# Down projection of a hybrid decoder trunk: 8 of 22 k-pairs by seven block products instead of eight; masks and query slots in pages, x in DRAM during the FFN

## The chip, the cores and the metric

One Trainium2 chip, one core of it. The metric is the time of one execution in device microseconds, median of several runs. PE is TensorE, DVE is VectorE, ACT is ScalarE, POOL is GpSimd, SP is SyncE, which here only issues DMAs.

## The reference

Two layers on x (256 x 2048, f32): layer 0 has a dilated attention mixer, layer 1 a sparse attention mixer, and each ends with a SwiGLU feed-forward. D_FF is 5632. What the change touches most is the product with `w_down`:

```python
def swiglu(u, w_gu, w_down):
    gu = u @ w_gu
    return (jax.nn.silu(gu[..., :D_FF]) * gu[..., D_FF:]) @ w_down
# per layer: x = x + rmsnorm(mixer(rmsnorm(x, g[0])), g[1])
#            x = x + rmsnorm(swiglu(rmsnorm(x, g[2]), ffn_w_gu[l], ffn_w_down[l]), g[3])
```

## The kernel before

Every f32 product is done in three passes at PE's rounded f32 type: a number is split into `hi` (rounded) and `lo` (the rest), and hi·hi, lo·hi and hi·lo are summed in PSUM. The weights come in **units** of 128 x 1024 f32 (512 KB). A unit's way is the same everywhere: SP loads it (`dma_one`, L182), ACT writes hi (L193), DVE writes lo = raw - hi (L194), both in `split_one`, and PE reads hi and lo. `_unit_list` writes the order of all units down by hand. `take`, called by PE's loops for the next unit, keeps loads and splits ahead of PE in program order: up to `NRAW` loaded units that are not split yet, and splits up to `look` units ahead, if enough pages are free (`room`, `st["res"]`).

SBUF is handed out in **pages** of 4 KB per partition (`Pages`, `NPAGE` = 44), first in, first out: raw, hi, lo, the activations' hi/lo pairs (`XT`, one page for a k-pair, i.e. two k-tiles of 128), x (4 pages), the tail's products `og` (4) and gain rows `gb` (2). PSUM's 8 banks are handed out the same way.

Side work (attention heads, evacuations) is written as generators. `spawn` queues one, `tick` (one per product, two in `x_unit`) advances them, so their instructions fall between PE's products in program order.

In `ffn`, gate/up comes first: per f-pair two banks (token tile 0 and 1), 8 units each; `gu_evac` makes h = silu(g)·u, transposes it on PE (L808) and splits it into `hT` (L812, L813). The **down projection** then runs over 4 column chunks of 512. A chunk has 22 units, one k-pair each; `x_unit` does for each of 2 k-tiles and 2 token tiles three matmuls of 128x512 (L330 to L332), 12 for a unit, into two banks. `Tail.chunk` squares a chunk's result for the RMSNorm (L563) and multiplies it by the gain (L567). The last chunk holds back 4 units (`HOLD`), does them for token tile 0 and then for tile 1 (`Tail.last`), so that most of the end lies beside matmuls; then come the factor r_o (L358 on DVE, L359 on POOL) and the residual (L597). During chunk 3, `step_f` of layer 0 loads and splits the memory tokens for layer 1 (L383, L384). After layer 0's FFN `next_x` transposes the new x (L608) between the matmuls of `mem_k`.

The attention masks lie in a constant tile `cst` of 128 x 1848 f32, loaded once at the start; the query slots, `vc` and `pcT` are tiles of their own.

## Time and profile before

| | |
|---|---|
| median of 3 runs | 2556.78 us (2556.25 to 2558.38) |
| the profiled execution's own time | 2556.86 us |
| its span in the profile | 2555.1 us |
| PE, PEld, DVE, ACT, POOL busy | 2522.1, 2137.7, 1449.6, 1203.3, 58.5 us |
| DMA | 482.84 MB, 189 GB/s in the mean |

Busy time of PE counts each matmul from its issue to its last result, and these overlap (a 128x512 takes about 390 ns and the next starts 227 ns after it), so rates are read from starts, not from means. The chain of work that ended last lies to 93% on PE, 4% on DVE, 2% on ACT.

### The profile page before, as it was taken

The page shows a single profiled execution, that of the slowest core. Times are in us where ns is not written, and L with a number is a line of the kernel's source. Part 1 is how long each engine was busy: PE and PEld are TensorE (multiplying, and loading weights), DVE is VectorE, ACT ScalarE, POOL GpSimd, SP SyncE. Part 2 cuts the span into 40 slices and gives each one's busy share as a digit, 9 for nine tenths or more (in the row PEclk, how much of TensorE's full clock was granted, in tenths as well). Part 3 has the DMA queues.
Part 4 walks back from the last instruction along what each step waited for, and adds up shares of the span by engine and source line. Part 5 has one row for each costly group of instructions (what it writes and reads, how often), then busy time and mean ns, then how long its engine had stood idle before and what let it go on. Part 6 is the DMA issues. An engine that isn't in the chain of part 4 may idle for free.

```text
span 2555.1 us, 32090 instructions
## 1 busy us (share of the span) xinstructions
PE 2522.1 (99%) x12326; PEld 2137.7 (84%) x12326; DVE 1449.6 (57%) x1926; ACT 1203.3 (47%) x1704; POOL 58.5 (2%) x73
## 2 busy tenths in 40 slices
PE   8999999999999999999999999999899999999998
PEld 6899999988888888888888888888788888888887
DVE  8564655557445554444457866896544444444444
ACT  7444444456434444444445555565444444444442
POOL 5000000000000000000000000000000000000000
PEclk9999999999999999999999999999999999999999
DMA  8455555576555555566676675346455555556664
GB/s 305 148 181 173 166 166 173 172 246 223 177 183 181 185 187 170 173 209 192 194 233 216 220 245 193 116 142 235 158 175 181 181 174 173 181 173 219 193 190 156
DMA packets 136010, 482.84 MB, mean 189 GB/s; under 512 B 15408, under 2 KB 15408, under 8 KB 135856
## 3 DMA queue, kind: packets, MB, share of 16 engines
q1 hardware_dynamic: 131904, 468.67, 56.8%
q0 software_dynamic: 3232, 11.01, 1.3%
q8 instruction: 96, 1.57, 0.3%
q10 hardware_dynamic: 720, 1.11, 0.1%
q14 instruction: 58, 0.48, 0.1%
HBM read 478.63 MB, written 2.10 MB: 188 GB/s over the span
## 4 chain that ended last, share of the span: by engine, by line
PE 93%; DVE 4%; ACT 2%; issue 1%; DMA 0%; POOL 0%; SPq 0%; DVEq 0%; ACTq 0%; POOLq 0%
PE bk L331 23%; PE bk L332 23%; PE bk L330 23%; PE bk L295 12%; PE bk L297 6%; DVE lo L194 2%; ACT hi L193 1%; PE sk L808 1%; PE sk L500 1%; PE bk L939 1%; PE bk L938 1%; PE sk L540 0%; PE bk L294 0%; PE sk L1123 0%; DVE x L597 0%
## 5 line engine op out<-in xcount | busy, mean ns | idle before, releaser
L194 DVE TENSOR_TENSOR lo<-raw,hi 128x1024 fp32r<-128x1024 f32 (+2 forms) x899 | 1061.6, 1205 | 613.0 <-ACT hi L193 575.6
L193 ACT ACTIVATE hi<-raw 128x1024 fp32r<-128x1024 f32 (+2 forms) x899 | 906.9, 1039 | 499.5 <-PE bk L331 239.3
L330 PE MATMUL bk<-hi,xf 128*128 128x512 f32 x1408 | 554.0, 393 | 0.6 <-ACT xf L383 0.6
L332 PE MATMUL bk<-lo,xf 128*128 128x512 f32 x1408 | 549.3, 390 | 0.0
L331 PE MATMUL bk<-hi,xf 128*128 128x512 f32 x1408 | 548.9, 390 | 0.0
L295 PE MATMUL bk<-xT,hi 128*128 128x512 f32 x1104 | 398.7, 404 | 0.0
L332 PEld LDWEIGHTS bk<-lo,xf 128*128 128x128 f32 x1408 | 265.0, 188 | 55.7
L330 PEld LDWEIGHTS bk<-hi,xf 128*128 128x128 f32 x1408 | 265.1, 188 | 54.1 <-ACT xf L383 1.0
L331 PEld LDWEIGHTS bk<-hi,xf 128*128 128x128 f32 x1408 | 265.3, 188 | 53.5 <-DVE xf L384 0.2
L297 PE MATMUL bk<-xT,lo 128*128 128x256 f32 x1035 | 289.6, 280 | 0.0
L330 PE MATMUL bk<-hi,hT 128*128 128x512 f32 x704 | 274.1, 389 | 0.0
L332 PE MATMUL bk<-lo,hT 128*128 128x512 f32 x704 | 273.9, 389 | 0.0
L331 PE MATMUL bk<-hi,hT 128*128 128x512 f32 x704 | 273.9, 389 | 0.0
L295 PEld LDWEIGHTS bk<-xT,hi 128*128 128x128 f32 x1104 | 204.1, 188 | 39.8 <-issue 0.2
L297 PEld LDWEIGHTS bk<-xT,lo 128*128 128x128 f32 x1035 | 195.5, 189 | 3.1
L331 PEld LDWEIGHTS bk<-hi,hT 128*128 128x128 f32 x704 | 132.2, 188 | 27.6
L330 PEld LDWEIGHTS bk<-hi,hT 128*128 128x128 f32 x704 | 132.2, 188 | 27.3
L332 PEld LDWEIGHTS bk<-lo,hT 128*128 128x128 f32 x704 | 132.2, 188 | 27.3
L801 DVE SCALAR_TENSOR_TENSOR ev<-bk,r_f,ev 128x256 f32<-128x256 f32 x88 | 42.2, 483 | 136.7 <-ACT ev L799 127.8
L799 ACT ACTIVATE ev<-bk,r_f 128x256 f32<-128x256 f32 x88 | 41.5, 474 | 164.9 <-PE bk L332 163.8
L322 ACT ACTIVATE ev<-bk 128x256 f32<-128x256 f32 x93 | 35.5, 382 | 129.7 <-PE bk L295 129.6
L295 PE MATMUL bk<-kT,hi 128*128 128x512 f32 x256 | 91.6, 399 | 0.0
(210 smaller groups left out, 2486.6 us busy)
## 6 DMA issues: line engine op xcount, KB each, us to landing
...
```

The lines of the kernel that those rows point to most:

```text
L193: nc.scalar.activation(hi[1][:, s], r[:, s], AF.Copy)
L194: nc.vector.tensor_tensor(out=lo[1][:, s], in0=r[:, s], in1=hi[1][:, s].bitcast(F32), op=OP.subtract)
L295: mm(pt[:, :], lhsT=hi[:, ks], rhs=X.hl(kt), start=first, stop=last)
L297: mm(pt[:, S:], lhsT=lo[:, ks], rhs=X.part(kt, 0), start=False, stop=False)
L322: nc.scalar.activation(t1, pt[1][:, S:], AF.Copy)
L330: mm(p[:, :w], lhsT=xh, rhs=u[0][1][:, ws], start=f, stop=False)
L331: mm(p[:, :w], lhsT=xl, rhs=u[0][1][:, ws], start=False, stop=False)
L332: mm(p[:, :w], lhsT=xh, rhs=u[1][1][:, ws], start=False, stop=l)
L500: mm(s[:, o:o + n], lhsT=q[1][:, g, t * P:(t + 1) * P], rhs=k[1][:, g, :n], start=True, stop=True)
L799: nc.scalar.activation(g, pts[t][1][:, :S], AF.Silu, scale=r)
L801: nc.vector.scalar_tensor_tensor(h, pts[t][1][:, S:], r, g, op0=OP.mult, op1=OP.mult)
L808: nc.tensor.transpose(p[:, k * S + t * P:k * S + (t + 1) * P], hs[t][:, k * P:(k + 1) * P], ident)
```

## The change

**Seven products.** For the k-pairs 14 to 21 (`DN_S`) the 2 token tiles, 2 k-tiles and 2 column chunks of a pair of chunks (cp 0: chunks 0 and 1; cp 1: chunks 2 and 3) form a 2x2x2 block product, done in Winograd's form with 7 products of three matmuls instead of 8. The sums of activation blocks are made once per k-pair in `gu_evac` (`s_parts`), kept in `sp` pages and in the place of the block they replace. The sums of weight blocks are made by DVE at each use: of units a (chunk 2cp) and b (chunk 2cp+1), each with halves A and B (its two k-tiles), DVE forms b.A - a.A and b.B - b.A in a page `T13`, and from it a.A + b.B - b.A, and a.B less that, in a's own raw page, `T24`; both are split like units. Seven banks hold the products and an eighth (`Q`) the ordinary part of the block (chunk 1, tile 1). A k-pair of this kind is called a quad here: four `take`s (a, b, T13, T24), 21 matmuls. The other 14 k-pairs go as before (kinds a and b), woven between the quads; chunk pairs replace single chunks. `sums` and `block` put the products together on DVE (L1061 to L1067, L1074).

**Pages.** Masks, query slots, `vc` and `pcT` move into pages of the layer that needs them (`work_a`, `work_b`, `work_free`), loaded by POOL's queue; `cst` shrinks to 128 x 252. x is stored to DRAM after `next_x` of each FFN and loaded again in cp 1; `gb` takes one page at a time, `og` pages are taken when used; `NPAGE` is 48.

```diff
-NPAGE = 44
+NPAGE = 48
+DN_S = tuple(range(14, FT // 2))
+def _dn_steps(cp):
+    std = [u for u in range(FT // 2) if u not in DN_S]
+    a, b, q = [("a", u) for u in std], [("b", u) for u in std], [("S", u) for u in DN_S]
+    if cp == 0:
+        head, mix, tail = a[:4], [e for p in zip(a[4:], b) for e in p] + b[len(a) - 4:], []
+        tail, mix = mix[-4:], mix[:-4]
+    else:
+        head, mix, tail = a[:3], a[3:] + b[:6], b[6:]
+    return head + _weave(mix, q, 0) + tail
...
     def split_one():
...
+        if kd == "b":
+            ai, ra = kept["T24"]
+            hl = pages.get([P, UNIT], F32R, "hl", True)
+            split_ap(r[:, Bk], hl[1][:, A], hl[1][:, Bk])
+            ti, t = pages.get([P, UNIT], F32, "t13", True)
+            nc.vector.tensor_tensor(out=t[:, A], in0=r[:, A], in1=ra[:, A], op=OP.subtract)
+            nc.vector.tensor_tensor(out=t[:, Bk], in0=r[:, Bk], in1=r[:, A], op=OP.subtract)
...
+        if kd == "T13":
+            ai, ra = kept["T24"]
+            nc.vector.tensor_tensor(out=ra[:, A], in0=r[:, Bk], in1=ra[:, A], op=OP.add)
+            nc.vector.tensor_tensor(out=ra[:, Bk], in0=ra[:, Bk], in1=ra[:, A], op=OP.subtract)
         for s in halves(u, w):
+            split_ap(r[:, s], hi[1][:, s], lo[1][:, s])
...
     def next_x(tail, x, X, g, res, name, w=3):
...
+        if name == "f":
+            for i in range(4):
+                nc.sync.dma_start(out=x_out[i], in_=x[i][1])
+                pages.put(x[i][0])
...
+    def s_parts(p, H, u):
+        nc.scalar.activation(a21, A[:, 0, 1], AF.Copy)
+        tt(out=sv[:, 0], in0=A[:, 1, 1], in1=a21, op=OP.add)
...
+        for h, l, v in todo:
+            nc.scalar.activation(h, v, AF.Copy)
+            tt(out=l, in0=v, in1=h.bitcast(F32), op=OP.subtract)
...
+            def quad(u):
+                w = take(f"dn{l}")
+                prod("P1", act(2 * u, 0), w[0][1][:, A], w[1][1][:, A])
+                prod("P2", act(2 * u + 1, 0), w[0][1][:, Bk], w[1][1][:, Bk])
+                w = take(f"dn{l}")
+                prod("P3", sp[3], w[0][1][:, A], w[0][1][:, Bk])
+                w = take(f"dn{l}")
+                prod("P5", sp[0], w[0][1][:, A], w[1][1][:, A])
+                prod("P7", sp[2], w[0][1][:, Bk], w[1][1][:, Bk])
+                w = take(f"dn{l}")
+                prod("P6", sp[1], w[0][1][:, A], w[1][1][:, A])
+                prod("P4", act(2 * u + 1, 1), w[0][1][:, Bk], w[1][1][:, Bk])
...
+            def block(key, pre=None):
+                c, t, s_ = T["c"][key]
+                nc.vector.tensor_tensor(out=s_, in0=bk[key][1], in1=s_, op=OP.add)
+                free(key)
+                tail.rows(2 * cp + c, t, s_, pre)
...
+                    if 8 <= steps < 12:
+                        i = steps - 8
+                        x[i] = pages.get([P, 1024], F32, "x")
+                        nc.sync.dma_start(out=x[i][1], in_=x_out[i])
```

Three places where the order of instructions changes. PE in layer 0's down projection before, the first half of a unit (three matmuls per token tile; `bk` are the banks):

```order
L330 MATMUL bk_9302<-hi_9265,hT_6056 128x512
L331 MATMUL bk_9302<-hi_9265,hT_6056 128x512
L332 MATMUL bk_9302<-lo_9266,hT_6056 128x512
L330 MATMUL bk_9303<-hi_9265,hT_6056 128x512
L331 MATMUL bk_9303<-hi_9265,hT_6056 128x512
L332 MATMUL bk_9303<-lo_9266,hT_6056 128x512
```

PE in layer 0's down projection after, the third to sixth of the seven products of the first quad (`hl` holds hi and lo of half a unit, `sp` the sums of activations):

```order
L1019 MATMUL bk_9546<-hl_9469,sp_8232 128x512
L1020 MATMUL bk_9546<-hl_9469,sp_8232 128x512
L1021 MATMUL bk_9546<-hl_9469,sp_8232 128x512
L1019 MATMUL bk_9552<-hi_9489,hT_8188 128x512
L1020 MATMUL bk_9552<-hi_9489,hT_8188 128x512
L1021 MATMUL bk_9552<-lo_9490,hT_8188 128x512
L1019 MATMUL bk_9556<-hi_9489,sp_8232 128x512
L1020 MATMUL bk_9556<-hi_9489,sp_8232 128x512
L1021 MATMUL bk_9556<-lo_9490,sp_8232 128x512
L1019 MATMUL bk_9568<-hi_9507,sp_8232 128x512
L1020 MATMUL bk_9568<-hi_9507,sp_8232 128x512
L1021 MATMUL bk_9568<-lo_9508,sp_8232 128x512
```

Before, two banks take turns every three matmuls; now every product of a quad goes to a bank of its own, still three matmuls for each, and one product of the eight is gone.

DVE at the start of layer 0's down projection before: the last transposed k-pair and the splits of five units.

```order
L813 TENSOR_TENSOR hT_9283<-sk_9328,hT_9283 128x2x256
L194 TENSOR_TENSOR lo_9358<-raw_9312,hi_9357 128x1024
L194 TENSOR_TENSOR lo_9376<-raw_9314,hi_9375 128x1024
L194 TENSOR_TENSOR lo_9394<-raw_9341,hi_9393 128x1024
L194 TENSOR_TENSOR lo_9412<-raw_9361,hi_9411 128x1024
L194 TENSOR_TENSOR lo_9430<-raw_9379,hi_9429 128x1024
```

DVE there after: the first quad from its unit b on, and the next two units (`t` is the page T13, and `raw` on the left the page that becomes T24).

```order
L233 TENSOR_TENSOR hl_9469<-raw_9370,hl_9469 128x512
L248 TENSOR_TENSOR t_1371_9472<-raw_9370,raw_9368 128x512
L249 TENSOR_TENSOR t_1371_9472<-raw_9370 128x512
L258 TENSOR_TENSOR raw_9368<-t_1371_9472,raw_9368 128x512
L259 TENSOR_TENSOR raw_9368<-raw_9368 128x512
L233 TENSOR_TENSOR lo_9490<-t_1371_9472,hi_9489 128x1024
L233 TENSOR_TENSOR lo_9508<-raw_9368,hi_9507 128x1024
L233 TENSOR_TENSOR lo_9524<-raw_9388,hi_9523 128x1024
L233 TENSOR_TENSOR lo_9530<-raw_9442,hi_9529 128x1024
```

Before, a unit is one instruction of DVE; a quad, two units, is eight: a split of a (ahead of the piece), half a split of b, four block sums and two splits of the sums.

DVE at the end of the run before (layer 1's down projection), from the factor of token tile 0 to the last residual:

```order
L358 TENSOR_SCALAR s_20500<-ssq,s_20472 128x1
L567 TENSOR_TENSOR og_18922<-bk_20148,gb_18918 128x512
L597 SCALAR_TENSOR_TENSOR x_4896<-og_18921,r_o,x_4896 128x512 x2
L597 SCALAR_TENSOR_TENSOR x_4898<-og_18922,r_o,x_4898 128x512 x2
L358 TENSOR_SCALAR s_20537<-ssq,s_20472 128x1
L567 TENSOR_TENSOR og_18924<-bk_20149,gb_18918 128x512
L597 SCALAR_TENSOR_TENSOR x_4900<-og_18923,r_o,x_4900 128x512 x2
L597 SCALAR_TENSOR_TENSOR x_4902<-og_18924,r_o,x_4902 128x512
```

The same place on DVE after:

```order
L1074 TENSOR_TENSOR og_20949<-bk_20303,og_20949 128x512
L427 TENSOR_SCALAR s_21054<-ssq,s_21025 128x1
L671 TENSOR_TENSOR og_20949<-og_20949,gb_20234 128x512
L710 SCALAR_TENSOR_TENSOR x_20831<-og_20120,r_o,x_20831 128x512 x2
L710 SCALAR_TENSOR_TENSOR x_20849<-og_20949,r_o,x_20849 128x512 x2
L1074 TENSOR_TENSOR og_20950<-bk_20756,og_20950 128x512
L427 TENSOR_SCALAR s_21092<-ssq,s_21025 128x1
L671 TENSOR_TENSOR og_20950<-og_20950,gb_20234 128x512
L710 SCALAR_TENSOR_TENSOR x_20869<-og_20121,r_o,x_20869 128x512 x2
L710 SCALAR_TENSOR_TENSOR x_20916<-og_20950,r_o,x_20916 128x512
```

A sum of 128x512 (L1074) now stands ahead of each of the two factors, and it is what the squares on ACT wait for.

## Rows read from the trace of the kernel before

**Rows 1.** The page of the profile: the engines' busy times, and the granted TensorE clock in 40 slices (9 is 90% or more).

```profile
PE 2522.1 (99%) x12326; PEld 2137.7 (84%) x12326; DVE 1449.6 (57%) x1926; ACT 1203.3 (47%) x1704; POOL 58.5 (2%) x73
...
PEclk9999999999999999999999999999999999999999
```

**Rows 2.** Busy time of each engine by stretch (us from the span's start: its length; PE, PEld, DVE, ACT, POOL busy with counts of instructions; granted clock; DMA share; GB/s). Gate/up of layer 0; down projection of layer 0; what follows it; the output projection's end in layer 1; down projection of layer 1; the end.

```profile
626.00:1117.00 491.00, 489.93 (x2201) 405.26 (x2201) 243.03 (x242) 213.45 (x251) 1.66 (x3) 1.00 0.58 185
1117.00:1356.50 239.50, 239.50 (x1061) 198.38 (x1060) 124.16 (x121) 104.75 (x121) 5.40 (x10) 1.00 0.65 205
1356.50:1440.00 83.50, 80.82 (x459) 69.48 (x458) 65.73 (x96) 49.17 (x77) 4.04 (x9) 1.00 0.63 216
...
1800.00:1830.00 30.00, 22.35 (x98) 17.24 (x97) 17.33 (x36) 17.21 (x32) 1.62 (x3) 0.83 0.39 132
...
2306.00:2546.00 240.00, 240.00 (x1063) 198.76 (x1062) 114.71 (x103) 96.83 (x103) 1.09 (x2) 1.00 0.60 190
2546.00:2555.10 9.10, 0.54 (x3) 0.11 (x1) 3.89 (x5) 1.41 (x3) 2.24 (x2) 0.77 0.43 165
```

**Rows 3.** The waits of PE on other engines in the whole run (in total, times, the longest): the first, the second and the last of eleven.

```profile
PE sk L608 <- DVE x L597: 8.7, 5, 4.5
PE bk L330 <- ACT hi L193: 6.0, 1, 6.0
...
PE sk L1121 <- ACT pcT L1104: 0.3, 1, 0.3
```

**Rows 4.** PE's timeline in layer 0's down projection (start, length): the first and the last row of a run of 31 matmuls.

```profile
1344.01 0.39 PE L330 MATMUL bk<-hi,hT 128*128 128x512 f32 x1
...
1350.81 0.39 PE L330 MATMUL bk<-hi,hT 128*128 128x512 f32 x1
```

**Rows 5.** Instructions of layer 0's down projection by line (1117 to 1356 us: count, busy us, mean ns; idle time before them and what ended it).

```profile
L194 DVE TENSOR_TENSOR lo<-raw,hi 128x1024 fp32r<-128x1024 f32 x88 | 107.7, 1225 | 104.1 <-ACT hi L193 103.7
L193 ACT ACTIVATE hi<-raw 128x1024 fp32r<-128x1024 f32 x88 | 92.6, 1058 | 111.6 <-PE bk L331 97.9 <-PE bk L332 9.2 <-DMA raw<-in_dn 3.0
...
L384 DVE SCALAR_TENSOR_TENSOR mT<-xraw,gains,mT 128x256 fp32r<-128x256 f32 x16 | 7.1, 483 | 5.7 <-ACT mT L383 5.7
L567 DVE TENSOR_TENSOR og<-bk,gb 128x512 f32<-128x512 f32 x7 | 4.8, 690 | 2.1 <-ACT junk L563 2.0
```

**Rows 6.** DVE's instructions of the whole run by line and shape (count, busy us, mean ns, idle before).

```profile
L194 DVE TENSOR_TENSOR lo<-raw,hi 128x1024 fp32r<-128x1024 f32 x833 | 1003.4, 1226 | 613.0 <-ACT hi L193 575.6 <-PE bk L331 28.4 <-issue 1.4
...
L1057 DVE SCALAR_TENSOR_TENSOR bp<-cst,sk 128x128 f32<-128x128 f32 x24 | 5.7, 278 | 0.0
...
L194 DVE TENSOR_TENSOR lo<-raw,hi 128x512 fp32r<-128x512 f32 x2 | 1.3, 692 | 0.0
```

**Rows 7.** ACT's, in the same form.

```profile
L193 ACT ACTIVATE hi<-raw 128x1024 fp32r<-128x1024 f32 x833 | 857.0, 1055 | 499.5 <-PE bk L331 239.3 <-PE bk L332 213.3 <-DVE lo L194 17.0
...
L193 ACT ACTIVATE hi<-raw 128x512 fp32r<-128x512 f32 x2 | 1.2, 624 | 0.0
```

**Rows 8.** DVE's timeline in the B mixer: two splits of 128x1024 back to back (start, length of both).

```profile
1599.13 2.36 DVE L194 TENSOR_TENSOR lo<-raw,hi 128x1024 fp32r<-128x1024 f32 x2 [5.47 <-ACT hi L193]
```

**Rows 9.** DVE in the first 40 us by line, where POOL adds squares at the same time.

```profile
L384 DVE SCALAR_TENSOR_TENSOR mT<-xraw,gains,mT 128x256 fp32r<-128x256 f32 x16 | 13.2, 866 | 4.2 <-ACT mT L383 4.2
```

**Rows 10.** The busiest stretch for DMA, near the start, and one shortly after it (columns as in Rows 2).

```profile
16.00:24.00 8.00, 8.00 (x35) 6.04 (x34) 8.00 (x8) 6.36 (x11) 7.17 (x4) 1.00 1.03 410
...
80.00:100.00 20.00, 20.00 (x114) 17.61 (x113) 12.67 (x27) 10.86 (x25) 0.00 (x0) 1.00 0.40 125
```

**Rows 11.** The end of the run on PE, ACT, DVE and POOL, in that order (start, length, [idle before <- releaser]).

```profile
2546.15 0.39 PE L332 MATMUL bk<-lo,hT 128*128 128x512 f32 x1
...
2546.64 0.60 ACT L563 ACTIVATE junk<-bk 128x512 bf16<-128x512 f32 x1 [4.81 <-PE bk L332]
2547.13 0.19 ACT L563 ACTIVATION_READ_ACCUMULATOR junk<-bk 128x1 f32 x1
...
2542.81 2.74 DVE L597 SCALAR_TENSOR_TENSOR x<-og,r_o,x 128x512 f32<-128x512 f32 x4
2547.36 0.21 DVE L358 TENSOR_SCALAR s<-ssq,s 128x1 f32<-128x1 f32 x1 [1.80 <-ACT junk L563]
2547.49 0.68 DVE L567 TENSOR_TENSOR og<-bk,gb 128x512 f32<-128x512 f32 x1
2548.22 3.08 DVE L597 SCALAR_TENSOR_TENSOR x<-og,r_o,x 128x512 f32<-128x512 f32 x3
...
2547.65 0.54 POOL L359 TENSOR_TENSOR r_o<-s,mhalf 128x1 f32<-128x1 f32 x1 [4.87 <-DVE s L358]
```

**Rows 12.** PE's timeline behind layer 0's down projection.

```profile
1360.72 0.27 PE L608 MATMUL sk<-cst,x 128*128 128x128 f32 x1
1361.67 0.55 PE L608 MATMUL sk<-cst,x 128*128 128x128 f32 x3 [0.68 <-DVE x L597]
```

**Rows 13.** PE's timeline where it waits for the new x in layer 1: the wait, and the matmuls behind it.

```profile
1819.50 0.55 PE L608 MATMUL sk<-cst,x 128*128 128x128 f32 x3 [2.15 <-DVE x L597]
...
1820.60 0.63 PE L330 MATMUL bk<-hi,xf 128*128 128x512 f32 x1
1821.03 0.63 PE L331 MATMUL bk<-hi,xf 128*128 128x512 f32 x1
...
1824.00 0.40 PE L332 MATMUL bk<-lo,xf 128*128 128x512 f32 x1
```

More of the change, by code (lines that the diff above doesn't have):

```diff
@@ L92, in _gu_order, with _dn_order @@
     return [(f"gu{l}", c * n + u) for u in range(n) for c in range(2)] + [(f"gu{l}", i) for i in range(2 * n, FT * 4)]
+DN_S = tuple(range(14, FT // 2))
[8 more added lines that the diff above has]
+    return head + _weave(mix, q, 0) + tail
+def _dn_order(l):
+    n, o = FT // 2, []
+    for cp in range(2):
+        for kind, u in _dn_steps(cp):
+            ia, ib = 2 * cp * n + u, (2 * cp + 1) * n + u
+            if kind == "S":
+                o += [(f"dn{l}", ia, "a"), (f"dn{l}", ib, "b"), (f"dn{l}", ia, "T13"), (f"dn{l}", ia, "T24")]
+            else:
+                o.append((f"dn{l}", ia if kind == "a" else ib))
+    return o
 def _unit_list():
@@ L151, in drop, with drop_one @@
         self.gone += 1
+    def drop_one(self, k2):
+        self.pages.put(self.t[k2][0])
+        self.out.add(k2)
     def release(self):
-        while self.gone < len(self.t):
-            self.drop()
+        for k2 in range(self.gone, len(self.t)):
+            if k2 not in self.out:
+                self.pages.put(self.t[k2][0])
+        self.gone = len(self.t)
 @with_exitstack
@@ L211, in take @@
         for _ in range(0 if st["quiet"] else 2):
-            while st["dma"] < min(st["split"] + NRAW, n) and room(1):
+            while st["dma"] < n and len(raws) < NRAW and room(1):
                 dma_one()
@@ L215, in take @@
                 split_one()
-        while not st["quiet"] and st["dma"] < min(st["split"] + 4, n) and room(1):
+        while not st["quiet"] and st["dma"] < n and len(raws) < 4 and room(3):
             dma_one()
@@ L221, in give @@
     def give(u):
-        pages.put(u[0][0], True)
-        pages.put(u[1][0], True)
+        for e in u:
+            pages.put(e[0], True)
     side = []
@@ L253, in until @@
             n += 1
-            assert n < 1000
+            assert n < 1000, (sorted(banks.live.values()), len(pages.free) + len(pages.own), [e[0].__name__ for e in side], [e[0].gi_frame.f_lineno for e in side])
     def drain():
@@ L480, in mem_head, with work_page, work_a, work_b @@
         pages.put(ti)
+    work, mask, qs = [], {}, {"n": 0, "s": []}
+    def work_page(name):
+        work.append(pages.get([P, 1024], F32, name))
+        return work[-1][1]
+    def work_a():
+        m0, m1 = work_page("mask"), work_page("mask")
+        nc.gpsimd.dma_start(out=m0[:, :768], in_=a["mask_a"][:, :768])
+        nc.gpsimd.dma_start(out=m1[:, :384], in_=a["mask_a"][:, 768:])
+        mask.update({0: m0[:, :384], 1: m0[:, 384:768], 2: m1[:, :384]})
+        qs["s"] = [m0[:, 768:], m1[:, 384:640], m1[:, 640:896]]
+    def work_b():
+        m, q, r = work_page("mask"), work_page("q"), work_page("pcT")
+        nc.gpsimd.dma_start(out=m[:, :NMASK_B], in_=a["mask_b"])
+        mask["b"], mask["vc"] = m, m[:, 512:]
+        nc.gpsimd.memset(m[:, 512:], 0.0)
+        nc.gpsimd.memset(r[:, :768], 0.0)
+        mask["pcT"] = [r[:, i * S:(i + 1) * S] for i in range(3)]
+        qs["s"] = [q[:, i * S:(i + 1) * S] for i in range(4)] + [r[:, 768:]]
+    def work_free():
+        while work:
+            pages.put(work.pop()[0])
+    def q_slot():
+        qs["n"] += 1
+        return qs["s"][qs["n"] % len(qs["s"])]
     sl_a = slopes(len(GROUPS) * AH)
@@ L599, in release @@
         def release(self):
-            for i, _ in self.og:
+            for i, _ in self.og.values():
                 pages.put(i)
@@ L608, in transposed @@
                 nc.tensor.transpose(p[:, k * S + t * P:k * S + (t + 1) * P], x[2 * t + kt // 8][1][:, hs], ident)
+    x_out = [dram.tile([P, 1024], F32, tag=f"x{i}", name=f"x{i}") for i in range(4)]
     def next_x(tail, x, X, g, res, name, w=3):
@@ L813, in gu_evac @@
         nc.vector.tensor_tensor(out=hp[:, :, 1, :], in0=pv, in1=hp[:, :, 0, :].bitcast(F32), op=OP.subtract)
+        if f2 in DN_S:
+            Sp[f2] = yield from s_parts(p, H, f2)
         banks.put(b)
@@ L841, in ffn @@
+        pair(0)
+        pair(1)
+        tail.finish()
         H.release()
+        st["look"] = 4
         return tail
@@ L919, in k_win @@
         return k_page(1)[:, 272 + g * S:272 + (g + 1) * S] if g < 2 else k_page(2)[:, g - 2, :]
[L922 to L926 removed]
+    work_b()
+    vc = mask["vc"].rearrange("p (g d) -> p g d", g=BG)
     def cmp_unit(i, u):
```

296 lines of the change are left out of this document (230 added, 66 removed).

## The prediction, made before the change was run

> **What bounds the kernel now.** I read the page first: PE is busy for 99% of the span at the full granted clock, DVE for 57% and ACT for 47% [rows 1]. The table by stretch says the same where the change lies: in both down projections PE is busy for the whole stretch, 239.50 of 239.50 us and 240.00 of 240.00, at clock 1.00, while DVE has 124.16 and 114.71 us of work, ACT 104.75 and 96.83, and DMA is 65% and 60% busy [rows 2]. The list of waits agrees: PE waits for others some 24 us in the run, 8.7 of them at the residual x between stages and 6.0 at the very start; none of the eleven kinds of wait is for a split of a down projection unit [rows 3]. The splits of those 88 units follow their producers at leisure: DVE idles 104 us before them for ACT's hi, and ACT 98 us before hi for PE, which has yet to free a page [rows 5]. So the down projection lasts as long as its matmuls need to issue, and a matmul taken away there is time taken away, provided that DVE and ACT still deliver.
>
> **What a matmul is worth.** Its row says 389 ns, but that is a latency. From 1344.01 to 1350.81 us there are 30 starts, so one costs 6.80 / 30 = 0.2267 us [rows 4]. I take this.
>
> **Step 1, the removed products.** 2 layers x 2 chunk pairs x 8 quads, one product of three matmuls less in each: 96 matmuls, 96 x 0.2267 = **-21.8 us**, all of it on PE's path. The other products keep their shape (128x128 weights, 512 columns) and their three matmuls for one bank, as before. The Trainium skill, page "TensorE: Matmul & The Clock Gate", section "Back-to-back issue gap", gives another price: 2.5 ns plus columns over 2.4 GHz, 215.8 ns, for a lone matmul and some 131 ns sustained, by which the 96 would be worth 20.7 or 12.6 us and the time would be 2537.6 or 2545.7 us. The measured distance in this very stage is above both, and decides.
>
> **Step 2, what DVE has to do for a quad.** Splits of 1024 columns at 1.226 us and of 512 at 0.692 us [rows 6]; the four block sums have the nearest row in that 512-wide split, too (f32, two operands in SBUF). A quad: 3 x 1.226 + 0.692 + 4 x 0.692 = 7.14 us, against 2.45 us for its two units before. These durations overlap in a queue: two 1024-wide splits take 2.36 us together, the second 1.14 us behind the first [rows 8]; by the same 0.09 us a 512-wide one is about 0.60, and the quad 6.42 us. PE needs 21 x 0.2267 = 4.76 us for the quad, so DVE falls behind by 1.7 to 2.4 us in it, and must make that up in the ordinary units woven between, where PE needs 12 x 0.2267 = 2.72 us and DVE 1.14 to 1.23.
> In cp 0 there are 20 units to 8 quads, 2.5 for one: PE 11.56 us, DVE 9.3 to 10.2 (80 to 88%). In cp 1 there are two: PE 10.20, DVE 8.7 to 9.6 (85 to 94%). ACT stays low: 5 x 1.055 + 0.624 = 5.9 us of 10.20 [rows 7]. Splits stand three to five units ahead of PE in program order; a part that is split five ahead may begin when PE begins the fifth before it. With two units, a, b, T13, T24 begun by PE at 0, 2.72, 5.44, 6.80, 7.48, 8.84 us and so on from 10.20, DVE may begin the next b at 7.48, has it (1.80 us) at 9.3 and T13 (2.34) at 11.6, and PE wants them at 17.0 and 17.7: some 6 us to spare. So I cost this at nothing. Its cover is the two ordinary units between quads.
> Tightest are two places. At the start of cp 1 the four blocks of cp 0 come first, each a sum and a product with the gain at 0.690 us [rows 5], 5.5 us; then DVE needs 1.23 + 2.07 + 2.61 us to have T13 ready, 11.4 us in all at full durations, and PE wants it after four units, P1, P2 and P3, 10.88 + 2.04 = 12.9 us: 1.5 us to spare. In layer 0's cp 1 the memory tokens add 2 x 0.483 us [rows 5] at every second step; in the worst period, around the last quad, two such steps make 9.6 + 1.9 = 11.5 us against 10.20, which the lead of about 6 us pays.
>
> **Step 3, the sums of activations.** `s_parts` adds per k-pair four 128-wide DVE operations on PSUM (0.278 us each by the nearest row [rows 6]) and splits of 128 and 384 columns, at most 0.3 and 0.7: some 2.1 us, in a stretch of gate/up in which DVE works 243 of 491 us [rows 2]. Hidden; if not, the first quad waits, since the last k-pair's sums are needed only at the eighth.
>
> **Step 4, the ends.** The last product is now followed by a sum of 128x512 on DVE before ACT can square: 0.690 us [rows 5] plus one hand-over of 0.04 (ACT's accumulator row ends at 2547.32, DVE's next begins at 2547.36 [rows 11]). In layer 1 this lies on the path: **+0.7 us**. Token tile 0 gets the same, but its residuals end at 2545.55 now and would at 2546.3, before the last matmul's end at 2546.54 [rows 11]. In layer 0 PE already waits 0.68 us for the residual [rows 12], so the same sum adds **+0.7 us** there.
>
> **Step 5, DMA and pages.** Weight traffic is the same. x goes out and back in each layer: 4 x 2.1 MB. The worst stretch is the one of cp 1 in which x comes back: two quads and two units, 15.0 us, with six unit loads and four of x of 0.52 MB and two of memory tokens of 0.26, 5.8 MB or 385 GB/s. The queues have moved 410 [rows 10], and three or four raw units lie ready in front of it. Nothing. SP waits for x to be final before it stores it and for a freed page before it loads it, with raw loads queued behind; but at both places the loads for the next eight or so units have been issued. Nothing. `cst` is 0.82 MB smaller at the start: at 410 GB/s the loads behind it come 2.0 us sooner, but DVE works 8.00 of 8.00 us there [rows 10] and is what PE waits for. Between 0 and -2.0 us I take 0. The masks come later, when DMA is 40% busy [rows 10]. The 48 pages less 2 or 3 for masks leave every other stage at least as many as it had.
>
> **The sum.** -21.8 + 0.7 + 0.7 = -20.3 us. The profiled execution took 2556.86 us, its span 2555.1 and 1.8 around it, and 2556.86 - 20.3 = 2536.6; it lies 0.08 above the median, so **2536.5 us**. Faster or slower by 0.2%, 5.1 us, is what a measurement of this kernel can tell from no change.
>
> **Rivals.**
> *Part of it comes back as waits in the quads* (10%). For it: the starts of cp 1 with 1.5 us to spare, DVE at 94% behind them. Against it: the lead elsewhere. A wait costs more than itself: behind an idle 2.15 us at 1819.50, eight matmuls from 1820.60 to 1824.00 were 0.43 us apart instead of 0.23 [rows 13], the lower clock, 1.6 us. Waits of 1 to 2 us with that, at two to four places: 2541 to 2549 us.
> *The distance between matmuls grows in the products* (5%, about no change). If a product of its own bank, weights and moving tile costs more than the alternation of two banks now, the 32 x 21 = 672 matmuls need 0.259 us instead of 0.227 to eat the 21.8 us: 2552 to 2562. Against it: two banks already change every three matmuls at 0.2267.
> *DVE becomes the bound, slower* (5%). Two SBUF operands are what the block sums read; an operation of that engine with f32 operands in SBUF took 0.866 us in the first 40 us, where POOL computes beside it, against 0.483 later [rows 5, 9]. In the down projection POOL works 5.4 of 239.5 us [rows 2], so there is no such neighbour. It would decide from where a quad costs DVE more than 10.20 - 2 x 1.14 = 7.9 us, 0.9 for each 512-wide operation. At 1.14, as for twice the width, a quad is 9.1 us, and a period 11.4 in cp 1 and 12.0 in cp 0: 16 x 1.2 + 16 x 0.4 = 26 us lost, 2563 us, and up to 50 more if PE drops to the lower clock at every quad.
> *The clock falls in the quads, slower* (2%). At the lower spacing of 0.427 us [rows 13] the 672 matmuls would take 134 us more, 2671. The whole run holds 1.00 wherever PE is fed, and drops only behind waits [rows 1, 2]. The same page of the Trainium skill, section "A second HAM failure mode: psum-queue depth-cycling", reports a kernel that cycled through PSUM banks and lost its clock between groups of matmuls, which is what seven banks in turn look like; this trace has no such case.
>
> **How the numbers follow.** The forecast has 78%, and alone spans 2534.5 (the start gains its 2.0 us) to 2541. The range 2534 to 2549 takes in the first rival; 12% lie above. Faster: 78 + 10 = 88%; within 0.2%: 5%; slower: 5 + 2 = 7%.
>
> **What would show it.** PE has 12,326 - 96 = 12,230 matmuls, still 0.227 us apart in the quads; each down projection lasts about 11 us less (228.6 us) with PE idle under 1 us and clock 1.00. DVE's busy time grows by 32 x 4.7 for quads, some 22 for sums and blocks and 34 for `s_parts`, to about 1660 us, ACT's by less than 100. The first wait behind the last matmul is 0.7 us longer. Waits of PE for lo (the split) or for a block sum's T13 or T24 in the down projections, or clocks under 1.00 there, would prove a rival right. If the down projections shrink by 22 us and the time does not, another stage has paid.

## The result, and the profile after

The changed kernel takes **2532.91 us** (median of four runs, 2531.84 to 2533.12) against 2557.5 for the kernel before (four runs, 2556.25 to 2558.38): ratio 0.9903, 95% interval 0.9886 to 0.9921. Its profiled execution took 2532.82 us with a span of 2531.0. The forecast was 2536.5, the range 2534 to 2549: faster as forecast, but by 24.0 us between the two profiled executions instead of 20.3, and 1.1 us below the range.

The page of the changed kernel, which answers to [rows 1]: 96 matmuls fewer, DVE 170 us busier, ACT 51, and the clock as before.

```profile
PE 2498.8 (99%) x12230; PEld 2119.4 (84%) x12230; DVE 1619.9 (64%) x2254; ACT 1254.8 (50%) x1828; POOL 59.2 (2%) x74
...
PEclk9999999999999999999999999999999999999999
```

Its busy times by stretch, with the columns of [rows 2]: gate/up of layer 0, the two halves (cp 0, cp 1) of the down projection of layer 0, those of layer 1, the end.

```profile
625.20:1115.70 490.50, 489.43 (x2199) 404.81 (x2198) 254.69 (x291) 218.81 (x278) 1.67 (x3) 1.00 0.56 189
1115.70:1222.00 106.30, 106.30 (x472) 88.03 (x471) 91.15 (x103) 59.06 (x65) 0.00 (x0) 1.00 0.63 200
1222.00:1344.60 122.60, 122.60 (x542) 101.51 (x542) 108.04 (x134) 69.52 (x92) 5.71 (x10) 1.00 0.69 240
2291.60:2398.00 106.40, 106.40 (x473) 88.08 (x472) 87.92 (x101) 58.57 (x65) 0.00 (x0) 1.00 0.62 203
2398.00:2520.70 122.70, 122.70 (x542) 101.31 (x540) 98.43 (x115) 57.80 (x72) 1.40 (x2) 1.00 0.55 192
2520.70:2531.00 10.30, 0.04 (x1) 0.00 (x0) 4.69 (x7) 1.44 (x3) 2.66 (x2) 0.68 0.50 170
```

Both down projections are 229 us long, PE never idles in them, the clock stays at 1.00, and DVE is 80 to 88% busy. PE's waits in the whole run (as [rows 3]; first, second, last) hold nothing of the down projections, as before:

```profile
PE sk L721 <- DVE x L710: 7.0, 3, 3.3
PE bk L399 <- ACT hi L232: 6.3, 1, 6.3
...
PE sk L1421 <- DVE bp L1367: 0.3, 1, 0.3
```

PE's timeline in a quad of layer 1 (as [rows 4]; start, length): from the third product of a quad to the second product of the unit behind it eighteen matmuls start in 4.08 us, 0.2267 apart; each product of the quad goes to a bank of its own. The first of them, one in the middle, and the one behind them:

```profile
2330.18 0.39 PE L1019 MATMUL bk<-hl,sp 128*128 128x512 f32 x1
...
2332.22 0.39 PE L1019 MATMUL bk<-hi,sp 128*128 128x512 f32 x1
...
2334.26 0.39 PE L1019 MATMUL bk<-hi,hT 128*128 128x512 f32 x1
```

The quads did what was forecast; the rest came from stages that the quads don't touch. The stages in us, each from its first matmul's start in PE's timeline to the next one's, the first from the span's start, the last from the last matmul's start to the span's end (e1 to e12 are the experiments below, 44p and so on their numbers of pages; A mixer is the attention mixer of layer 0, kv and b_q the two parts of layer 1's):

```
stage                before   e12   after    e1   e2(44p) e5(46p) e9(47p)  e10     e7
start                 59.29  58.80  58.43  58.88   58.22   58.57   58.51  58.25  58.19
A mixer              470.09 470.20 470.54 470.61  470.54  470.54  470.73 470.56 470.73
a_out, memory values  97.11  97.11  96.24  96.23   96.24   96.23   96.23  97.20  96.22
gate/up 0            490.62 490.62 490.51 490.59  491.06  490.57  490.56 490.58 490.58
down 0               239.82 239.83 228.95 239.82  231.10  230.00  229.95 228.94 229.44
its end, mem. keys 1  27.42  27.40  27.84  27.07   28.19   28.19   27.84  27.85  27.09
kv                   165.65 165.68 164.77 164.79  167.07  165.48  164.77 164.76 164.86
b_q (mixer 1)        152.46 152.48 151.21 151.21  195.18  151.20  153.59 151.21 151.20
b_out and its end    104.82 104.81 103.77 103.40  104.32  104.90  103.45 103.76 103.77
gate/up 1            499.27 499.06 499.38 499.05  499.40  499.38  499.29 499.40 499.25
down 1 to last matm. 239.60 239.60 228.72 239.60  232.82  229.73  228.72 228.72 229.22
end                    8.95   9.41  10.64   9.45   10.66   10.91   10.76  10.67   9.45
```

Before against after: the down projections lost 10.87 and 10.88 us, 48 x 0.2267 each. The end gained 1.69. Start, a_out, kv, b_q and b_out lost 0.86, 0.87, 0.88, 1.25 and 1.05, together 4.91, which no step of the prediction holds.

The end of the run in the changed kernel on ACT, DVE and POOL, as [rows 11]; the last matmul started at 2520.36:

```profile
2521.59 0.63 ACT L665 ACTIVATE junk<-og 128x512 bf16<-128x512 f32 x1 [4.73 <-DVE og L1074]
2522.12 0.19 ACT L665 ACTIVATION_READ_ACCUMULATOR junk<-og 128x1 f32 x1
...
2520.81 0.68 DVE L1074 TENSOR_TENSOR og<-bk,og 128x512 f32<-128x512 f32 x1
2522.34 0.21 DVE L427 TENSOR_SCALAR s<-ssq,s 128x1 f32<-128x1 f32 x1 [0.85 <-ACT junk L665]
2522.47 0.68 DVE L671 TENSOR_TENSOR og<-og,gb 128x512 f32<-128x512 f32 x1
2523.59 3.08 DVE L710 SCALAR_TENSOR_TENSOR x<-og,r_o,x 128x512 f32<-128x512 f32 x3 [0.44 <-POOL r_o L428]
...
2522.64 0.93 POOL L428 TENSOR_TENSOR r_o<-s,mhalf 128x1 f32<-128x1 f32 x1 [4.52 <-DVE s L427]
```

ACT's square starts 1.23 us behind the last matmul's start instead of 0.49: the 0.7 forecast. But POOL's power (the factor r_o, which the residual L710 needs) takes 0.93 us instead of 0.54, and DVE waits for it. In layer 0's end PE waits 1.53 us for the residual, where [rows 12] had 0.68. POOL's power is as slow there, but the residual doesn't wait for it; it stands behind two splits, which end 2.1 us after the power does. POOL's and DVE's timelines there:

```profile
1346.70 0.93 POOL L428 TENSOR_TENSOR r_o<-s,mhalf 128x1 f32<-128x1 f32 x1 [4.55 <-DVE s L427]
...
1347.36 2.36 DVE L233 TENSOR_TENSOR lo<-raw,hi 128x1024 fp32r<-128x1024 f32 x2
1349.64 0.87 DVE L710 SCALAR_TENSOR_TENSOR x<-og,r_o,x 128x256 f32<-128x256 f32 x2
```

### The profile page after: what moved, and what is told of

It reads as the page before. It is cut to its first block, busy times and chain, and to the rows that moved or that the text cites. A ratio compares the mean times of both kernels' runs of the same rounds, so it can differ in the third digit from the quotient of the medians.

```text
span 2531.0 us, 32497 instructions
## 1 busy us (share of the span) xinstructions
PE 2498.8 (99%) x12230; PEld 2119.4 (84%) x12230; DVE 1619.9 (64%) x2254; ACT 1254.8 (50%) x1828; POOL 59.2 (2%) x74
## 4 chain that ended last, share of the span: by engine, by line
PE 93%; DVE 3%; ACT 2%; issue 1%; POOL 0%; DMA 0%; DVEq 0%; POOLq 0%; ACTq 0%
PE bk L399 17%; PE bk L400 17%; PE bk L401 17%; PE bk L364 12%; PE bk L1021 6%; PE bk L1019 6%; PE bk L1020 6%; PE bk L366 6%; DVE lo L233 2%; ACT hi L232 1%; PE sk L977 1%; PE sk L600 1%; PE bk L1249 1%; PE bk L1248 1%; DVE x L710 0%
## 5 line engine op out<-in xcount | busy, mean ns | idle before, releaser
L233 DVE TENSOR_TENSOR lo<-raw,hi 128x1024 fp32r<-128x1024 f32 (+2 forms) x899 | 1046.4, 1205 | 301.8 <-ACT hi L232 270.4
L232 ACT ACTIVATE hi<-raw 128x1024 fp32r<-128x1024 f32 (+2 forms) x899 | 886.1, 1035 | 169.7 <-PE bk L400 51.6
L1019 PE MATMUL bk<-hi,hT 128*128 128x512 f32 x576 | 224.3, 389 | 0.0
L1020 PE MATMUL bk<-hi,hT 128*128 128x512 f32 x576 | 224.1, 389 | 0.0
L1021 PE MATMUL bk<-lo,hT 128*128 128x512 f32 x576 | 224.1, 389 | 0.0
L1021 PEld LDWEIGHTS bk<-lo,hT 128*128 128x128 f32 x576 | 108.1, 188 | 22.5
L1020 PEld LDWEIGHTS bk<-hi,hT 128*128 128x128 f32 x576 | 108.1, 188 | 22.4
L1019 PEld LDWEIGHTS bk<-hi,hT 128*128 128x128 f32 x576 | 108.1, 188 | 22.3
L392 DVE TENSOR_TENSOR ev<-bk,ev 128x256 f32<-128x256 f32 x93 | 39.3, 422 | 91.7 <-ACT ev L391 91.0
```

Of the source, the lines that this page charges most:

```text
L232: nc.scalar.activation(hi, src, AF.Copy)
L233: nc.vector.tensor_tensor(out=lo, in0=src, in1=hi.bitcast(F32), op=OP.subtract)
L1019: mm(p, lhsT=xh, rhs=wh, start=f, stop=False)
L1020: mm(p, lhsT=xl, rhs=wh, start=False, stop=False)
L1021: mm(p, lhsT=xh, rhs=wl, start=False, stop=e)
```

## Experiments

Theory: the quads gave the 21.8 us and the longer ends and nothing else; the 4.9 us come from the other edits, which let the splits stand elsewhere in DVE's and ACT's order. Rival: they are the spread between two executions.

**All but the quads (e1).** The down projections with all their products again, in the order and with the page reserve of the kernel before, everything else as changed:

```diff
-DN_S = tuple(range(14, FT // 2))
+DN_S = ()
...
-        pair(0)
-        pair(1)
...
+        for c in range(4):
...
+                    if 8 <= u < 12:
+                        x[u - 8] = pages.get([P, 1024], F32, "x")
+                        nc.sync.dma_start(out=x[u - 8][1], in_=x_out[u - 8])
+                x_unit(pts, f"dn{l}", H, 2 * u, 512, u == 0, u == n - 1, c == 3)
```

> The change without its seven-product part: down projections with all their products again, but 48 pages, small constants at the start, masks in pages, x in DRAM, gains and products taken late. Theory (the other edits gain on their own, outside the down projections): the stages outside them start as in the changed kernel: memory's first w product at 33.3 us instead of 34.3, the first transposed x of layer 1's mixer some 136.6 us before b_out's end at no quad, B mixer 151.3 us long instead of 152.4; both down projections 239.5 and 240 us again. 2557 - 1.0 (start) - 0.9 (a_out) - 0.9 (r_x) - 1.1 (B mixer) - 1.1 (b_out) + 0.7 (A mixer) = 2552.7 us. Rival (these stage differences are the spread between two executions): 2556 to 2558 us. Rival (the quads' own order brings them): 2557 us, and the stage starts of the kernel before.

2552.4 us (2552.06 to 2553.18), ratio 0.9981 (0.9972 to 0.9991): the theory's 2552.7. Its stages agree too (column e1), except that the start is only 0.4 us shorter instead of 1.0. Quads apart, the change is worth some 5 us, and the two parts simply add up.

**44, 46 and 47 pages (e2, e5, e9).** One edit, `NPAGE = 48` to 44, 46, 47.

> The changed kernel with 44 pages instead of 48 (masks still in pages). Theory (page count sets how far splits run ahead in the B mixer and b_out): their gains go, so B mixer 152.4 us or more instead of 151.3, the PE wait at the end of b_out 4.5 instead of 3.3 us, the start (33.3 us) and a_out keep theirs: 2532.9 + 2.2 to 3.1 = 2535 to 2536 us; the quads still gain 10.9 us in each layer. Rival (not the pages but the start, x in DRAM or late-taken pages): 2533 us, b_out's wait still 3.3 us. Rival (the quads need the pages): PE waits for lo or T13 inside the down projections, over 2538 us.

2586.05 us, ratio 1.0111 (1.0096 to 1.0126), 53 us above the changed kernel: no theory had this. Some 44 of it lie in b_q. (The second rival was right in a small part: the down projections are 2.2 and 4.1 us longer, and PE waits 3.1 us in them for hi and lo.) The row of b_q by stretch, with the columns of [rows 2]:

```profile
1542.40:1737.60 195.20, 170.71 (x900) 143.17 (x898) 122.88 (x354) 95.84 (x235) 0.53 (x1) 0.92 0.33 111
```

PE's waits there:

```profile
PE bk L364 <- ACT hi L232: 14.2, 11, 1.7
PE bk L366 <- DVE lo L233: 8.9, 12, 1.1
PE bk L399 <- ACT hi L232: 1.4, 1, 1.4
```

In the program's order the splits stand 0 to 1 units ahead of PE there, 2 to 3 with 48 pages. PE idles 24.5 us for hi and lo, its granted clock falls to 0.92 in the mean, and the same matmuls are busy for 170.7 us instead of 151.3 as in the changed kernel, whose row for b_q is

```profile
1537.20:1688.50 151.30, 151.30 (x901) 133.36 (x900) 120.81 (x351) 93.45 (x232) 0.53 (x1) 1.00 0.42 143
```

The masks and query slots take three pages from this mixer: with 44 in all, as before, the change makes the kernel slower.

> The changed kernel with 46 pages. In program order the splits of layer 1's mixer then stand 1 to 2 units ahead of PE, as in the kernel before (0 to 1 with 44 pages, 2 to 3 with 48). Theory (the lead, set by the pages that are left beside the masks, is what moved the stages of layer 1): the b_q stage lasts about 152.4 us as before the change, kv about 165.7, b_out about 104.8, memory's keys 27.5: about 3 us over the changed kernel, 2536 us. Rival (the price jumps with the first page lost): PE waits for hi in b_q with lower clock, 2545 us or more. Rival (lead does not matter until it is 0): 151.2 us and 2533 us.

2537.5 us (one run). The down projections are 1.0 us longer each, memory's keys 28.19. kv 165.48 as forecast, b_out 104.90 as forecast, but b_q 151.20. So the lead did not shorten b_q: with 46 pages it is as small as before the change, and b_q is short all the same. Nor is b_out's excess the old wait: PE waits 1.39 us, 17 us into it, for a head's bp (0.27 in the changed kernel), while at its end it waits 3.3 us as in the changed kernel, not 4.5 as in [rows 3].

> The changed kernel with 47 pages. In program order its splits then stand 2 units ahead of PE in b_q, more than with 46 pages (1 to 2), but they are issued in the bunches of the kernel before: 4 at the last memory query unit, where 44, 46 and 48 pages give 3. Theory (b_q's 1.25 us came from a bunch that got one split smaller, so that DVE reaches a memory head's softmax one split earlier): the b_q stage lasts 152.4 us here, as before the change, though it lasts 151.2 with 46 and with 48 pages; b_out 103.4 to 103.8, kv about 165; 2534 us. Rival (the lead itself, or masks in pages, or x in DRAM): 151.2 us, 2533 us.

2536.13 us (one run), b_q 153.59 us: longer with 47 pages than with 46 or 48, as only the theory of bunches had it (a bunch: splits issued in one piece, with nothing else of DVE between them), though 1.2 more than it said. PE's waits there:

```profile
PE sk L1280 <- ACT hidT L1266: 0.8, 1, 0.8
PE sk L539 <- DVE mp L534: 0.7, 1, 0.7
PE sk L1431 <- ACT pcT L1414: 0.3, 1, 0.3
```

DVE's timeline there (start, length):

```profile
1573.98 3.50 DVE L233 TENSOR_TENSOR lo<-raw,hi 128x1024 fp32r<-128x1024 f32 x3 [1.73 <-ACT hi L232]
1577.39 0.68 DVE L523 TENSOR_REDUCE nm<-sk 128x2 f32<-128x512 f32 x1
```

and with 48 pages, where PE waits for nothing in this stage:

```profile
1572.62 2.36 DVE L233 TENSOR_TENSOR lo<-raw,hi 128x1024 fp32r<-128x1024 f32 x2 [1.61 <-ACT hi L232]
1574.90 0.68 DVE L523 TENSOR_REDUCE nm<-sk 128x2 f32<-128x512 f32 x1
```

Three splits stand ahead of a softmax's maximum (L523) instead of two; what follows from it, down to hidT on ACT, comes one split, 1.14 us, later. The kernel before has the same bunch of three, at the same place, and the same waits for hidT and pcT (0.7 and 0.3 us):

```profile
1585.36 3.50 DVE L194 TENSOR_TENSOR lo<-raw,hi 128x1024 fp32r<-128x1024 f32 x3 [1.57 <-ACT hi L193]
```

It has no wait for mp; that one, 0.7 us, is the larger part of the 1.2 us more.

**The page that the first split takes (e10).** In the kernel before, the first split behind a_out takes the page of the second gain half, whose last reader, DVE's product with the gain, stands behind a_out's last matmul. ACT's timeline there:

```profile
601.63 2.01 ACT L193 ACTIVATE hi<-raw 128x1024 fp32r<-128x1024 f32 x2 [0.88 <-DVE og L567]
```

First I undid the late taking of pages (e6):

```diff
             self.gain(0)
+            if name == "a":
+                self.gain(1)
+                self.og = {i: pages.get([P, 1024], F32, "og") for i in range(4)}
```

> The changed kernel with both gain pages and the four product pages of layer 0's mixer tail taken at once, as before, instead of one by one. Theory (the late taking gave a_out's end its 0.9 us, since a split no longer waits for a page that DVE still works on): the stage from the first matmul of a_out to the first of gate/up lasts 97.1 us again instead of 96.2, ACT's hi waits 0.9 us for DVE there; 2533.8 us. Rival (masks in pages or x's traffic did it): 96.2 us.

2532.28 us (one run), a_out 96.23: the theory fell. a_out is as short with 44, 46 and 47 pages, so it isn't their number either; the list of free pages has another order in the changed program. So e10 put that very page first:

```diff
         mv[l] = pages.get([P, 2, 512], F32, "mv")
+        if l == 1:
+            pages.free.remove(tail.gb[1][0])
+            pages.free.insert(0, tail.gb[1][0])
```

> The changed kernel in which the first split of the stage behind layer 0's mixer takes the page that held the second gain half, as it does in the kernel before, instead of the page that has been free longest. Theory (a_out's 0.9 us came from that page: its last reader is the product with the gain on DVE, which stands behind the last matmul): ACT's hi waits 0.9 us for DVE again, PE waits 0.9 us at the first transposes of x, and the stage from a_out's first matmul to gate/up's lasts 97.1 us instead of 96.2. Rival (masks or x): 96.2 us.

a_out 97.20 us; 2533.65 (one run). ACT's timeline there in e10, then in the changed kernel:

```profile
601.07 2.00 ACT L232 ACTIVATE hi<-raw 128x1024 fp32r<-128x1024 f32 x2 [0.88 <-DVE og L671]
```

```profile
600.26 2.00 ACT L232 ACTIVATE hi<-raw 128x1024 fp32r<-128x1024 f32 x2
```

The 0.9 us are one page's identity: shown.

**The start (e4, e12).** e4 loads as many constants as before; e12 is the kernel before with its mask columns loaded later (first and second diff).

```diff
     nc.sync.dma_start(out=cst, in_=a["consts"])
+    for name, n in (("mask_a", 1024), ("mask_b", 444)):
+        pad = pages.get([P, 1024], F32, "pad")
+        nc.sync.dma_start(out=pad[1][:, :n], in_=a[name][:, :n])
...
```

```diff
-    nc.sync.dma_start(out=cst, in_=a["consts"])
+    nc.sync.dma_start(out=cst[:, :C_DA], in_=a["consts"][:, :C_DA])
+    nc.sync.dma_start(out=cst[:, C_J:], in_=a["consts"][:, C_J:])
...
+    nc.gpsimd.dma_start(out=cst[:, C_DA:C_J], in_=a["consts"][:, C_DA:C_J])
```

> The changed kernel with as many bytes of constants loaded at the start as before (0.82 MB more on SP's queue behind the first weights, into two pages that are otherwise unused there). Theory (the smaller constants gave the start its 1.0 us): the first w product of the memory stage starts at 34.3 us instead of 33.3, ACT's wait for the first raw load of the memory's weights is 2.85 instead of 1.67 us, and every later stage follows 1.0 us later: 2533.9 us. Rival (DVE bounds the start whatever the loads do, and the 1.0 us came from elsewhere): 33.3 us, 2532.9 us.

2534.35 us (2532.89 to 2534.79), ratio 0.9909 (0.9894 to 0.9924); the start lasts 60.41 instead of 58.43: the sign is right, the size twice that forecast, and ACT's wait for the first whole unit is 1.90 us, not 2.85. (The profiled execution, 2534.79 us, is the slowest of the four, 1.9 us above the fastest.)

> The kernel before, with only the mask columns of its constants (0.82 MB) loaded later, on POOL's queue at the start of the memory queries. Theory (those bytes in front of the weights gave the start its 0.9 us): the first x product comes at 58.1 to 58.9 us, as in every kernel with short constants, instead of 59.29. All stages behind it last as in the kernel before, and the repeat shows how far they can be trusted: mixer 470.09, a_out 97.11, kv 165.65, b_q 152.46, b_out 104.82 us: 2556.0 us. Rival (execution to execution spread): 59.3 us, or other stages off by as much as the 0.9 to 1.25 us.

2556.75 us (one run), start 58.80, 0.5 less than before; ACT's wait is still 2.75 us. Eleven traces with short constants and the changed kernel's program have 58.06 to 58.88. ACT's wait goes from 1.10 to 2.62 us in them, so it doesn't follow the constants. By these two runs the bytes cost 0.5 to 2.0 us, in a start that spreads by 0.8 on its own: the sign is likely, the size is not shown. The stages of e12 between the start and the end repeat those of before within 0.21 us, a_out, kv, b_q and b_out within 0.03: the rival, spread, is out for those four.

**The end (e3, e7).** In e3 the product with the gain is issued ahead of the factor 1/rms:

```diff
-            if pre is not None:
-                rstd_of(pre, self.ssq[:, t, c:c + 1], t, self.r)
...
             nc.vector.tensor_tensor(out=self.og[pg][1][:, hs], in0=src, in1=self.gb[c // 2][1][:, hs], op=OP.mult)
+            if pre is not None:
+                rstd_of(pre, self.ssq[:, t, c:c + 1], t, self.r)
```

> The changed kernel with the product with the gain issued on DVE ahead of the factor 1/rms in the last block of each token tile. Theory (POOL's power took 0.93 instead of 0.55 us because it ran beside a DVE operation with two SBUF operands): the product now runs while ACT squares, the power takes 0.55 us again, and the wait behind the last matmul falls by 0.4 us at the end of each layer, 2532.9 - 0.8 = 2532.1 us, 0.4 of it seen at the end of the run. Rival (the power is slow for another reason): it stays at 0.9 us; then at most 0.1 us is gained.

2533.75 us (2533.54 to 2534.0), ratio 0.9907 (0.9893 to 0.9922): no gain, and the end is 0.9 us longer (11.54). The timeline of DVE and POOL at the end of e3 (L669 is the product):

```profile
2522.49 0.69 DVE L669 TENSOR_TENSOR og<-og,gb 128x512 f32<-128x512 f32 x1 [0.85 <-ACT junk L665]
2523.10 0.21 DVE L427 TENSOR_SCALAR s<-ssq,s 128x1 f32<-128x1 f32 x1
...
2523.39 0.54 POOL L428 TENSOR_TENSOR r_o<-s,mhalf 128x1 f32<-128x1 f32 x1 [5.12 <-DVE s L427]
```

The power is short again, 0.54 us, without the product beside it; but the product writes the page that ACT's square still reads, so it couldn't start earlier, and stood in the way. e7 lets PE add the sum to the bank:

```diff
...
+                split_ap(sq, sp[1][:, :512], sp[1][:, 512:])
...
+                    if t:
+                        for h in range(2):
+                            mm(bk["Q"][1], lhsT=idr, rhs=sp[1][:, h * 512:(h + 1) * 512], start=False, stop=False)
```

> The changed kernel with the last block's sum s taken into its bank by PE: s is split into hi and lo (ACT, DVE, while PE works on the other token tile), and two matmuls with the identity add them ahead of the last 24; then ACT squares and DVE multiplies straight from the bank, as in the kernel before. Theory (the tail costs a sum of 0.69 us, a hand-over of 0.04 and 0.38 us of POOL's power beside a two-operand DVE operation): 2 x 0.2267 us more on PE and 1.1 less behind it, at the end of each layer: tail 10.64 - 1.1 = 9.5 us, power 0.55 us, 2532.9 - 1.3 = 2531.6 us. Rival (the power is slow because of its place, not its neighbour): tail 9.9 us, 2532.4 us.

2531.79 us (2531.77 to 2531.84), ratio 0.9900 (0.9885 to 0.9914) to the kernel before, as forecast (2531.6); its highest run is as low as the changed kernel's lowest. End 9.45 us, layer 0's end 0.75 shorter, each down projection 0.5 longer. It is the fastest version here. It holds both kinds of neighbour in one trace. The timeline of DVE and POOL at its end, token tile 0 (product of two SBUF operands) and 1 (of a bank and SBUF):

```profile
2516.71 0.68 DVE L671 TENSOR_TENSOR og<-og,gb 128x512 f32<-128x512 f32 x1
...
2521.88 0.68 DVE L671 TENSOR_TENSOR og<-bk,gb 128x512 f32<-128x512 f32 x1
...
2516.94 0.87 POOL L428 TENSOR_TENSOR r_o<-s,mhalf 128x1 f32<-128x1 f32 x1 [114.26 <-DVE s L427]
2522.05 0.55 POOL L428 TENSOR_TENSOR r_o<-s,mhalf 128x1 f32<-128x1 f32 x1 [4.23 <-DVE s L427]
```

**More quads (e8, e11b).** `DN_S = tuple(range(12, FT // 2))`, ten quads; then nine (from 13), with e7's sum, for which e11b keeps two pages back while the last four units are fetched. Without that (e11) the 48 pages don't suffice for nine quads and e7's sum.

> The changed kernel with ten of 22 k-pairs by seven products instead of eight. Theory (a quad is worth 12 times 0.2267 us less over both layers, and DVE keeps up with one and a half ordinary units to a quad: 8.84 us of PE, 8.1 to 9.0 us of DVE): down projections 2.7 us shorter each, 226.2 and 226.0 us, 2532.9 - 5.4 = 2527.5 us, if the lead of splits before layer 1's mixer stays. Rival (DVE is the bound from here on): PE waits for lo, T13 or T24 in the down projections, 2530 us or more. Rival (the quads' pages, 7 to 8 instead of 6, take the lead of gate/up's last splits): waits in gate/up instead, 2529 to 2533 us.

2543.59 us, ratio 0.9947 (0.993 to 0.9963): slower by 10.7 than with eight, against a forecast of 5.4 faster. The down projections took 229.54 and 227.45 us (forecast 226.2 and 226.0), the stage behind layer 0's 36.55, 8.7 more than with eight; b_q is 2.4 longer, with the three waits of e9. PE's waits in e8 from layer 0's down projection to the start of kv:

```profile
PE sk L721 <- DVE x L710: 8.7, 2, 6.8
PE bk L1021 <- DVE lo L233: 1.6, 3, 0.7
```

DVE's timeline there:

```profile
1343.81 3.67 DVE L233 TENSOR_TENSOR lo<-raw,hi 128x1024 fp32r<-128x1024 f32 x3 [0.27 <-ACT hi L232]
...
1350.41 2.74 DVE L710 SCALAR_TENSOR_TENSOR x<-og,r_o,x 128x512 f32<-128x512 f32 x4 [0.46 <-POOL r_o L428]
1353.07 0.68 DVE L1074 TENSOR_TENSOR og<-bk,og 128x512 f32<-128x512 f32 x1
```

DVE comes late to the last blocks: the last matmul started at 1345.26, its block's sum 7.8 us later, behind three splits and the residuals of token tile 0. The rival was right: DVE is the bound. It shows inside layer 0's down projection too, where PE waits 1.6 us for lo, but most of it at the end.

> The changed kernel with nine quads instead of eight, and the last block's sum by PE (two pages are kept back for its hi and lo while the last four units are fetched). Theory (DVE's arrears at the end of layer 0's down projection, 6.8 us of PE waiting for the residual with ten quads, begin only beyond nine): down projections 1.36 us shorter each, 227.6 and 227.4 us plus 0.45 for the identity matmuls, 2531.8 - 2.7 = 2529.1 us. Rival (they begin with the ninth): PE waits 2 to 4 us for x at memory's keys in layer 1, 2531 to 2534 us.

2537.61 us, ratio 0.9923 (0.9906 to 0.9939): 5.8 over e7. Down projections 231.09 and 229.32 us instead of 229.44 and 229.22, kv 2.3 and b_q 2.3 longer. That is 8.5 above the forecast, and neither theory had it: the waits for x stayed small. The trace has e9's bunch of three splits and its three waits in b_q, and in kv a wait of 1.5 us for r_x, as in the kernel before, with a granted clock of 0.99. Whether the ninth quad or the two pages kept back brought them, no run tells.

## Why the prediction was wrong by 3.7 us

*The removed products* (step 1): right to 0.1 us. *What DVE has to do* (step 2) and *the sums of activations* (step 3): hidden, as forecast; DVE was 86 and 83% busy in cp 0 (forecast 80 to 88), 88 and 80% in cp 1 (forecast 85 to 94, for its quads). Busy time grew by 170 us to 1619.9, not to some 1660: I had too much for `s_parts` and the quads. e8 shows that the margin was real and thin: it is gone with ten. The rivals did not come: no wait in the quads, 0.2267 us between their matmuls, clock 1.00. Seven banks in turn did not cost the clock, and PE had no gaps between groups here. The Trainium skill, page "TensorE: Matmul & The Clock Gate", section "A second HAM failure mode: psum-queue depth-cycling", reports it lost in another kernel, which cycled through banks and had short idle times between its groups.

*The ends* (step 4): the mechanism was right, at the end of the run the size was too small. +0.74 us for the sum came as forecast at both ends; 0.4 more at the end of the run is POOL's power beside a product whose two operands now both lie in SBUF. I had priced that product as unchanged. In layer 0 the same slow power is hidden behind the two splits, and only 0.1 us came on top of the sum. The Trainium skill, page "SBUF — State Buffer", section "Who interferes with whom", says that such an instruction of DVE contends with one of POOL that reads SBUF; the rows agree in kind, 0.87 to 0.93 us against 0.54 to 0.55. The remaining half microsecond of the end's 1.69 lies behind the start of the last residuals; e12 shows a spread of that size there (9.41 us against 8.95, same code).

**The step that failed is step 5**, "The 48 pages less 2 or 3 for masks leave every other stage at least as many as it had", costed at nothing, with no bound below. It is not nothing: e1 shows 5 us outside the quads. But more pages are not by themselves what does it: of the five places only kv follows their number. What changed is which page a split gets (a_out: e10) and how many splits are issued in one piece ahead of work that PE waits for. In b_q these are three or two (e9). For kv they are the splits of the memory keys' second unit, between the residuals of x, two before and one now:

```profile
1361.93 2.35 DVE L194 TENSOR_TENSOR lo<-raw,hi 128x1024 fp32r<-128x1024 f32 x2
...
1350.43 1.22 DVE L233 TENSOR_TENSOR lo<-raw,hi 128x1024 fp32r<-128x1024 f32 x1
```

What hangs on them is r_x, POOL's factor 1/rms of x, for which PE waits in kv; its waits for it before and after are

```profile
PE sk L371 <- POOL r_x L359: 2.0, 2, 1.5
...
PE sk L440 <- POOL r_x L428: 1.1, 2, 0.7
```

With 46 pages two splits stand there and the longest wait is 1.5 us (kv 165.5); with 47 it is one split and 0.7 us, as with 48 (kv 164.8). From the end of PE's wait for the residual in layer 0's end to the end of its wait for r_x it is 29.9 us before and with 46 pages, 28.8 with 47 and in the changed kernel: one split, a part of which already falls into the memory keys (the 0.4 us below). Ahead of b_out's residual, too, there were two splits and is now one:

```profile
1803.00 2.36 DVE L194 TENSOR_TENSOR lo<-raw,hi 128x1024 fp32r<-128x1024 f32 x2
...
1789.12 1.23 DVE L233 TENSOR_TENSOR lo<-raw,hi 128x1024 fp32r<-128x1024 f32 x1
```

PE's wait for it fell from 4.5 to 3.3 us in every variant of the changed program, e1 among them. kv and b_out are read from order and trace together; no kernel changed them alone. Nor does any run take back alone one edit that helps to set this order: `take` now loads a fourth raw unit ahead only when three pages are free (`room(3)`), where one was enough before. What part of the order is its work and what part that of the pages stays open. The price of one split is 1.14 to 1.23 us of DVE [rows 6, 8], and the stages at these places moved by 0.9 to 1.25. The lead itself decided only where it came to nothing (e2).

The start's 0.9 us lay inside the 0 to -2.0 us that step 5 gave; taking 0, because DVE is busy there, was the wrong end, as far as a start that spreads by 0.8 us can tell. The account against -20.3: start, a_out, kv, b_q and b_out -4.9, memory keys -0.4, A mixer +0.45, the end +1.0, layer 0's end +0.15, together -3.7. The A mixer's 0.45, which every variant has and e12 has not, is no single wait: it grows over the whole mixer in steps of 0.1 us or less. Its cause stays open.

The range failed with it: its low end let only the start gain. With one split, 1.14 us, as a bound at three of the five waits for the residual [rows 3] it would have reached 2531.
